# A two-layer encoder on one core: waits placed behind a branch's first gates, and the neighbourhood values in two matmul passes instead of three

## The chip, the cores and the metric

The kernel runs on one NeuronCore of a Trainium2 chip (trn2). The metric is the device time of one execution in microseconds, as a median of several runs. Before the change it is 1117.35 us, the median of three runs from 1117.09 to 1117.47 us. The lines L1 to L1314 named below are those of the kernel before; where a line of the changed kernel is meant, the text says so.

## The reference

A two-layer encoder works on 256 tokens of width 1024. Each layer is a hybrid mixer, a cross-attention to a memory of 256 tokens, and a feed-forward block with a depthwise convolution, with a layer norm behind each. The change lies in the mixer, which merges three branches, each weighed by its own sigmoid gate:

```python
    oa = diff_attention(qa..., ka..., va..., lam, pos)
    ya = (rms_norm(oa, subln_g) * (1.0 - lam_init)).transpose(0, 2, 1, 3).reshape(b, s, DA_V)
    yb = neighbourhood_attention(qb, kb, vb, rpb)
    yc = gb * dwconv(gc * hc, sc_conv_w)
    g = jax.nn.sigmoid(gates.reshape(b, s, N_BRANCH, D_MODEL))
    merged = (g[:, :, 0] * (ya @ w_branch[0]) + g[:, :, 1] * (yb @ w_branch[1])
              + g[:, :, 2] * (yc @ w_branch[2]))
    return merged @ w_mix_out
```

`neighbourhood_attention` has 8 heads of 64. The tokens are a grid of 4 rows by 64 columns; a query sees 16 columns of all four rows. The kernel computes it as full 256 by 256 scores for each head with a bias that holds a large negative number outside the window, a softmax, and the product with the head's values:

```python
        sc = jnp.where(mask, sc + bias[None].astype(jnp.float32), -jnp.inf)
        p = jax.nn.softmax(...)
        return jnp.einsum('bhjqrk,bhrjkd->bhjqd', p.astype(v_blk.dtype), v_blk)
```

## The kernel before

**High and low parts.** The inputs are float32, and TensorE multiplies them as float32r, a rounded form. To keep precision, operands are split into a high part (a copy to float32r on ScalarE, L276) and a low part (the rest, on VectorE, L277) by `split_from`, and a product is made of three matmuls that add up in PSUM (`mm3`, L271 to L273): high times high, high times low, low times high. The weights arrive as 355 units of 128 by 1024 float32 (`raw`), are loaded by SyncE's DMA queue, and are split in the same way into `hi` and `lo`, up to seven units ahead of their use (`LOOK`, 8 buffers each).

**What sets the order.** The program is written as steps (`Step`) by generators. A planner, `interleave`, puts them in one list: a main line of projections, side lines that are spawned (attention groups, `Spawn`), and waits (`Wait`) that hold the main line until a side line is done by the planner's own costs. The list is then recorded, and the tile framework's scheduler may still move instructions on each engine before it fixes their order; on the chip each engine issues its own list in that order. PSUM has three buffers `acc` for projections and five `att` for attention and transposes; a buffer is taken again when its last reader is done.

**The mixer.** In each layer the main line runs the values, queries and keys of both attentions and the convolution branch, and then three calls of `branch`: first the convolution branch (br 2), then the differential attention (br 0), then the neighbourhood (br 1). A call does two halves of 512 output columns: four weight units of gate projection (`g`, matmuls of 512 columns into two `acc` tiles, one for each 128 tokens; a tanh on ScalarE evacuates each, L830), then two units of the branch product (`w`, two more `acc` tiles), which VectorE merges with the gate (L838, and L841 for the later branches). Ahead of the call for branch 0 stands `Wait(da)`, ahead of that for branch 1 `Wait(na0..na3)`.

**The neighbourhood.** Four side lines `near_pair` (t = 0 to 3, two heads each) run while the main line is in the first `branch` call. Each has scores for two heads (L587 and L588, then on VectorE bias, maximum, and after the exponent on ScalarE the division by the sum, L744 to L753), two transposes of the weights (L761, then a split into the t512 tiles `t` by L276 and L277), and `values`: for each of two heads j and two token tiles k one `mm3` of the values' high and low parts (`vh`, `vl`, 128 columns that hold both heads) with the transposed weights (256 queries), 12 matmuls of 256 columns into one `att` tile `po`. Of its 128 rows those of head j are used, and split to `yb` from PSUM, 64 rows by 256 columns at a time (two L276 and two L277 a pair).

## Time and profile before

| what | number |
|---|---|
| median of three runs | 1117.35 us (1117.09 to 1117.47) |
| the profiled execution's own time | 1118.29 us |
| its span | 1116.5 us |
| PE busy | 1096.6 us, 98% of the span, 6684 matmuls |
| weight loads of PE (PEld) | 980.5 us, 88% |
| DVE (VectorE) busy | 831.6 us, 74%, 1300 instructions |
| ACT (ScalarE) busy | 643.2 us, 58%, 1062 instructions |
| mean granted TensorE clock | 0.996 |
| share of PE in the chain that ended last | 91% |

The profiled execution is 0.94 us longer than the median. A matmul is shown with its whole duration, and matmuls overlap, so the distance between two starts is what one costs the engine. Names such as `acc<-hi,big` give the tile written and the tiles read, `att<-t,big` is a value product, `lo<-raw,hi` the low part of a weight unit. Layer 1 of the model repeats layer 0 some 540 us later.

### The profile page before, as it was taken

Reading aid. Unit: us, or ns where it says so; the run is one execution under the profiler, and the core shown is the slowest. Engines: PE = TensorE matmul, PEld = TensorE weight load, DVE = VectorE, ACT = ScalarE, POOL = GpSimd, SP = SyncE. Lnnn points to the kernel's source line nnn. Section 1 sums busy time; section 2 is a strip of 40 time slices with the busy share of each in tenths; the row PEclk is TensorE's granted clock in tenths of the full one; section 3 lists DMA queues with packets and bytes.
Section 4 is the critical chain, followed back from the end, with each engine's and each line's share of the span. In section 5 each row is a group of like instructions: output and inputs, shape, how many; then the busy total and the mean of one; then the engine's idle time right before and its main releaser. Section 6 shows DMA issues by size and latency. Waiting matters only on the chain.

```text
span 1116.5 us, 17399 instructions
## 1 busy us (share of the span) xinstructions
PE 1096.6 (98%) x6684; PEld 980.5 (88%) x6684; DVE 831.6 (74%) x1300; ACT 643.2 (58%) x1062; POOL 12.3 (1%) x18
## 2 busy tenths in 40 slices
PE   9999999999999999999999999999999989999997
PEld 7899998888998988888889999888889978888886
DVE  7787888666974988885586888865787658988744
ACT  5656767445553676664445667654546436766540
POOL 0000000000000000000000000000000000000001
PEclk9999999999999999999999999999999989999999
DMA  7884437567463576666747544566756516766651
GB/s 301 283 257 148 147 129 234 176 200 246 152 207 97 166 238 190 189 189 194 262 147 216 185 157 171 170 188 197 236 170 195 164 44 225 214 190 188 194 173 38
DMA packets 60466, 208.45 MB, mean 187 GB/s; under 512 B 7008, under 2 KB 8288, under 8 KB 60384
## 3 DMA queue, kind: packets, MB, share of 16 engines
q1 hardware_dynamic: 59952, 206.83, 57.6%
q8 instruction: 52, 0.85, 0.3%
q10 hardware_dynamic: 432, 0.52, 0.1%
q14 instruction: 30, 0.25, 0.1%
HBM read 204.18 MB, written 1.05 MB: 184 GB/s over the span
## 4 chain that ended last, share of the span: by engine, by line
PE 91%; DVE 3%; DMA 2%; ACT 1%; SPq 1%; issue 1%; DVEq 0%; ACTq 0%
PE acc L271 18%; PE acc L272 18%; PE acc L273 18%; PE acc L303 12%; PE acc L301 7%; PE att L272 4%; PE att L273 4%; PE att L271 4%; PE acc L299 2%; DMA raw<-in_w_dram 1%; PE att L462 1%; DMA big<-in_emb_ln_b_dram 1%; DVE lo L277 1%; PE att L673 1%; PE att L588 1%
## 5 line engine op out<-in xcount | busy, mean ns | idle before, releaser
L277 DVE TENSOR_TENSOR lo<-raw,hi 128x1024 fp32r<-128x1024 f32 x355 | 432.1, 1223 | 179.3 <-ACT hi L276 173.6
L276 ACT CAST hi<-raw 128x1024 fp32r<-128x1024 f32 x355 | 371.2, 1052 | 221.7 <-PE acc L273 72.8
L272 PE MATMUL acc<-lo,big 128*128 128x512 f32 x584 | 229.5, 393 | 0.8 <-DVE lo L277 0.8
L271 PE MATMUL acc<-hi,big 128*128 128x512 f32 x584 | 229.0, 394 | 0.4 <-ACT hi L276 0.4
L273 PE MATMUL acc<-hi,big 128*128 128x512 f32 x584 | 227.0, 391 | 0.0
L271 PE MATMUL acc<-big,hi 128*128 128x256 f32 x704 | 200.5, 286 | 3.2 <-ACT big L335 2.4
L273 PE MATMUL acc<-big,lo 128*128 128x256 f32 x704 | 200.8, 285 | 0.6 <-DVE lo L277 0.6
L272 PE MATMUL acc<-big,hi 128*128 128x256 f32 x704 | 200.2, 285 | 0.2 <-DVE big L277 0.2
L303 PE MATMUL acc<-big,hi 128*128 128x512 f32 x588 | 149.4, 393 | 0.0
L271 PEld LDWEIGHTS acc<-big,hi 128*128 128x128 f32 x704 | 134.8, 192 | 4.4 <-ACT big L335 2.8
L273 PEld LDWEIGHTS acc<-big,lo 128*128 128x128 f32 x704 | 135.0, 192 | 1.2 <-DVE lo L277 1.0
L272 PEld LDWEIGHTS acc<-big,hi 128*128 128x128 f32 x704 | 135.0, 192 | 0.8 <-DVE big L277 0.4
L273 PEld LDWEIGHTS acc<-hi,big 128*128 128x128 f32 x584 | 109.8, 188 | 22.8 <-DVE big L277 0.2
L272 PEld LDWEIGHTS acc<-lo,big 128*128 128x128 f32 x584 | 110.0, 188 | 21.7 <-DVE lo L277 1.9
L271 PEld LDWEIGHTS acc<-hi,big 128*128 128x128 f32 x584 | 109.8, 188 | 20.9 <-ACT hi L276 1.0
L303 PEld LDWEIGHTS acc<-big,hi 128*128 128x128 f32 x588 | 105.1, 189 | 18.3
L301 PEld LDWEIGHTS acc<-big,lo 128*128 128x128 f32 x672 | 91.8, 191 | 6.6 <-ACT big L276 0.2
L301 PE MATMUL acc<-big,lo 128*128 128x256 f32 x672 | 94.0, 283 | 0.0
L272 PE MATMUL att<-lo,big 128*128 128x256 f32 (+1 forms) x228 | 73.8, 324 | 0.0
L271 PE MATMUL att<-hi,big 128*128 128x256 f32 (+1 forms) x228 | 73.5, 322 | 0.0
L273 PE MATMUL att<-hi,big 128*128 128x256 f32 (+1 forms) x228 | 73.4, 322 | 0.0
L307 ACT COPY t<-acc 128x256 f32<-128x256 f32 x84 | 31.1, 370 | 59.0 <-PE acc L303 59.0
(155 smaller groups left out, 1237.7 us busy)
## 6 DMA issues: line engine op xcount, KB each, us to landing
raw<-in_w_dram SPq DMA_DIRECT2D x355, 512.0 KB, 4.3
t<-in_bias_dram SPq DMA_DIRECT2D x16, 256.0 KB, 5.2
big<-in_ln_g_dram SPq DMA_DIRECT2D x6, 512.0 KB, 5.4
big<-in_ln_b_dram SPq DMA_DIRECT2D x6, 512.0 KB, 6.2
raw<-in_memT_dram SPq DMA_DIRECT2D x6, 512.0 KB, 4.7
big<-big SPq DMA_DIRECT2D x16, 128.0 KB, 2.3
x<-in_x_dram SPq DMA_DIRECT2D x4, 256.0 KB, 7.5
t<-in_memT_dram SPq DMA_DIRECT2D x3, 256.0 KB, 6.6
```

The lines of the kernel that those rows point to most:

```text
L271: mm(o, lh, rh, start=first, stop=False)
L272: mm(o, lh, rl, start=False, stop=False)
L273: self.done = mm(o, ll, rh, start=False, stop=last)
L276: return (self.nc.scalar.copy(ah, src), self.nc.vector.tensor_tensor(out=al, in0=src, in1=rd(ah), op=ALU.subtract))
L277: self.nc.vector.tensor_tensor(out=al, in0=src, in1=rd(ah), op=ALU.subtract))
L299: mm(o, hi[:, 0], xa.both(0), start=True, stop=False)
L301: mm(o[:, S:], lo[:, k], xa.hi(k), start=False, stop=False)
L303: mm(o, hi[:, k], xa.both(k), start=False, stop=k == KT - 1)
L307: self.nc.scalar.copy(dst, o[:, S:])
L462: nc.tensor.transpose(pt[:, k], self.x[i][:, (n * h + k) * P:(n * h + k + 1) * P], self.ident)
L588: self.nc.tensor.matmul(o, q[m][:, h, t], k[2 + m][:, h], start=False, stop=True)
L673: self.nc.tensor.matmul(sh["po"][:, hd], st["wt"][:, h, k], va[:, 512 * k + hd * P:512 * k + (hd + 1) * P], start=k == 0, stop=k == 1)
```

## The change

**The operand.** The values of the neighbourhood, `vb`, are evacuated into one tile for each 128 tokens, in which each head has 128 columns: its 64 high columns, then its 64 low ones. One matmul with such a block as the stationary operand gives the high part's product in rows 0 to 63 and the low part's in rows 64 to 127. `values` runs two passes for each j and k, one with the weights' high part and one with their low part: 8 matmuls a pair in place of 12. The product low times low, which was left out, is now included.

**The evacuation.** The two halves of `po` are to be added: ScalarE copies the lower 64 rows by 512 columns from PSUM to a new t512 tile `y` (L782 of the changed kernel), VectorE adds the upper ones (L783), and the split to `yb` then reads `y` in SBUF (L786 on ScalarE, L787 on VectorE, two each, 64 by 256). A pair's chain of evacuation is ACT, DVE, ACT, DVE, where it was ACT, DVE.

**The waits.** `Wait(da)` and `Wait(na...)` move from ahead of a `branch` call to behind its first four gate units. The planner's cost of `values` goes from 1.3 to 0.96, its latency from 1.6 to 2.4. Other lines of the changed kernel stand 2 to 8 lines lower (L761 is L763, L838 is L846, L830 is L836).

The planner's list has 561 steps in both kernels, and they stand in the same order. SyncE's and GpSimd's instructions stand in the same order too. What moves is the order on PE, ACT and DVE near the value products, and a little around the norm and the first feed-forward units of layer 1.

```diff
--- before.py
+++ after.py
@@ -371,7 +371,9 @@
             if n not in self.T or self.T[n][0] != l:
                 self.T[n] = (l, [self.big(F32R), self.big(F32R)] if split else self.big())
             if split:
-                self.split_from(o, self.T[n][1][0][:, sl], self.T[n][1][1][:, sl])
+
+                v = self.T[n][1][i].rearrange("p (h s d) -> p h s d", s=2, d=64)
+                self.split_from(o.rearrange("p (h d) -> p h d", d=64), v[:, :, 0], v[:, :, 1])
             else:
                 self.nc.scalar.copy(self.T[n][1][:, sl], o)
         return self.tok(n, l, 0, xn, evac, tiles)
@@ -769,21 +771,25 @@
             if ("yb", l) not in self.T:
                 self.T["yb", l] = self.big_act(1)
             yb = self.T["yb", l]
-            vh, vl = self.T["vb"][1]
+
             po = self.att().rearrange("p (j t) -> p j t", j=2)
             for j in range(2):
                 for k in range(2):
-                    c = slice(512 * k + t * P, 512 * k + (t + 1) * P)
-                    wh, wl = st["w"][j]
-                    self.mm3(po[:, j], vh[:, c], vl[:, c], wh[:, k], wl[:, k], k == 0, k == 1)
+                    v = self.T["vb"][1][k][:, (2 * t + j) * P:(2 * t + j + 1) * P]
+                    for s in range(2):
+                        nc.tensor.matmul(po[:, j], v, st["w"][j][s][:, k], start=k == s == 0, stop=k == s == 1)
+            y = self.t512().rearrange("p (j t) -> p j t", j=2)
+            nc.scalar.copy(y[:64], po[64:])
+            nc.vector.tensor_tensor(out=y[:64], in0=po[:64], in1=y[:64], op=ALU.add)
             for j in range(2):
                 a = slice(64 * j, 64 * j + 64)
-                self.split_from(po[a, j], yb.his[0][a, t], yb.los[0][a, t])
+                nc.scalar.copy(yb.his[0][a, t], y[:64, j])
+                nc.vector.tensor_tensor(out=yb.los[0][a, t], in0=y[:64, j], in1=rd(yb.his[0])[a, t], op=ALU.subtract)
 
         yield Step(scores, 0.87, 4.0, acq=2, rel=2)
         yield Step(lambda: transp(0), 0.44, 1.4, acq=1, rel=1)
         yield Step(lambda: transp(1), 0.44, 1.8, acq=1, rel=1)
-        yield Step(values, 1.3, 1.6, acq=1, rel=1)
+        yield Step(values, 0.96, 2.4, acq=1, rel=1)
 
 
     def conv_branch(self, l, xn):
@@ -817,7 +823,7 @@
         yield from self.feat("gb", l, 4, xn, gb)
 
 
-    def branch(self, l, br, y, xn, first=False, last=False):
+    def branch(self, l, br, y, xn, first=False, last=False, waits=()):
 
         T = self.T
         for q in range(2):
@@ -829,6 +835,8 @@
 
                 self.nc.scalar.activation(gs[i], o, AF.Tanh, scale=0.5)
             yield from self.tok(f"g{br}", l, q, xn, gate)
+            if q == 0 and waits:
+                yield Wait(*waits)
 
             def merge(i, o, gs=gs, sl=sl):
                 nc = self.nc
@@ -1032,10 +1040,8 @@
             for t in range(4):
                 yield Spawn(f"na{l}{t}", self.near_pair(l, t), 1.0)
             yield from self.branch(l, 2, ("yc", l), xn, first=True)
-            yield Wait(f"da{l}")
-            yield from self.branch(l, 0, ("ya", l), xn)
-            yield Wait(*(f"na{l}{t}" for t in range(4)))
-            yield from self.branch(l, 1, ("yb", l), xn, last=True)
+            yield from self.branch(l, 0, ("ya", l), xn, waits=[f"da{l}"])
+            yield from self.branch(l, 1, ("yb", l), xn, last=True, waits=[f"na{l}{t}" for t in range(4)])
             yield lnc(0)
             yield Allow(max(allow["v", l, 0], allow["k", l, 7]))
             yield Step(self.load_mem)
```

PE, layer 0, the last pair (t = 3): `att_2179` and `att_2206` before (`att_2176` and `att_2203` now) are the transposed weights of its two heads, `att_2233` (`att_2230`) its `po`, and `acc_2285` (`acc_2281`) the second tile of the product of branch 2's second half. First the kernel before, then the changed one.

```order
L761 MATMUL att_2179<-ident,t_1942 128x128 x4
L761 MATMUL att_2206<-ident,t_1944 128x128 x4
L271 MATMUL att_2233<-t_2184,big_920 128x256
L272 MATMUL att_2233<-t_2185,big_920 128x256
L273 MATMUL att_2233<-t_2184,big_921 128x256
L271 MATMUL att_2233<-t_2184,big_920 128x256
L272 MATMUL att_2233<-t_2185,big_920 128x256
L273 MATMUL att_2233<-t_2184,big_921 128x256
L271 MATMUL att_2233<-t_2211,big_920 128x256
L271 MATMUL acc_2285<-hi_1978,big_1439 128x512
L272 MATMUL acc_2285<-lo_1979,big_1439 128x512
```

```order
L763 MATMUL att_2176<-ident,t_1942 128x128 x4
L763 MATMUL att_2203<-ident,t_1944 128x128
L780 MATMUL att_2230<-t_2181,big_920 128x256
L763 MATMUL att_2203<-ident,t_1944 128x128 x3
L780 MATMUL att_2230<-t_2182,big_920 128x256
L780 MATMUL att_2230<-t_2181,big_921 128x256
L780 MATMUL att_2230<-t_2182,big_921 128x256
L780 MATMUL att_2230<-t_2208,big_920 128x256
L780 MATMUL att_2230<-t_2209,big_920 128x256
L780 MATMUL att_2230<-t_2208,big_921 128x256
L780 MATMUL att_2230<-t_2209,big_921 128x256
L271 MATMUL acc_2281<-hi_1978,big_1439 128x512
```

Before, the first head's products and one of the second stand ahead of 12 matmuls into `acc`, and the other five behind them; now all eight stand ahead of the `acc` matmuls, the first of them among the transposes.

ACT at the same place: `t_2262` and `t_2270` (`t_2258` and `t_2266` now) are the gates of branch 2's second half, read from the `acc` tiles of the gate projection.

```order
L276 CAST hi_2274<-raw_2272 128x1024
L276 CAST big_2036<-att_2162 64x256
L276 CAST t_2184<-att_2179 128x512
L276 CAST big_2036<-att_2162 64x256
L276 CAST t_2211<-att_2206 128x512
L830 ACTIVATE t_2262<-acc_2148 128x512
L830 ACTIVATE t_2270<-acc_2155 128x512
L276 CAST hi_2294<-raw_2292 128x1024
L276 CAST hi_2314<-raw_2312 128x1024
L276 CAST big_2036<-att_2233 64x256
```

```order
L276 CAST hi_2270<-raw_2268 128x1024
L782 COPY t_2169<-att_2160 64x512
L276 CAST t_2181<-att_2176 128x512
L786 CAST big_2036<-t_2169 64x256 x2
L276 CAST t_2208<-att_2203 128x512
L782 COPY t_2239<-att_2230 64x512
L836 ACTIVATE t_2258<-acc_2146 128x512
L836 ACTIVATE t_2266<-acc_2153 128x512
L786 CAST big_2036<-t_2239 64x256 x2
L276 CAST hi_2290<-raw_2288 128x1024
```

The two tanh stood behind the copy of the second transposed head; now the copy of the last pair's `po` stands ahead of them. `acc_2281` takes the PSUM buffer of `acc_2146`, as `acc_2285` took that of `acc_2148`.

DVE ahead of that: the last rows before the division of the last head's weights, `t_1944` (L753, now L755), and what follows.

```order
L277 TENSOR_TENSOR lo_2218<-raw_2215,hi_2217 128x1024
L753 TENSOR_SCALAR t_1942<-t_1942,s_2088 128x256 x2
L277 TENSOR_TENSOR lo_2253<-raw_2250,hi_2252 128x1024
L751 RECIPROCAL s_2103<-s_2103 128x2
L277 TENSOR_TENSOR lo_2275<-raw_2272,hi_2274 128x1024
L277 TENSOR_TENSOR big_2037<-att_2162,big_2036 64x256
L753 TENSOR_SCALAR t_1944<-t_1944,s_2103 128x256 x2
L277 TENSOR_TENSOR t_2185<-att_2179,t_2184 128x512
L277 TENSOR_TENSOR big_2037<-att_2162,big_2036 64x256
L277 TENSOR_TENSOR t_2212<-att_2206,t_2211 128x512
```

```order
L277 TENSOR_TENSOR lo_2215<-raw_2212,hi_2214 128x1024
L277 TENSOR_TENSOR lo_2249<-raw_2246,hi_2248 128x1024
L753 RECIPROCAL s_2101<-s_2101 128x2
L277 TENSOR_TENSOR lo_2271<-raw_2268,hi_2270 128x1024
L783 TENSOR_TENSOR t_2169<-att_2160,t_2169 64x512
L755 TENSOR_SCALAR t_1944<-t_1944,s_2101 128x256 x2
L277 TENSOR_TENSOR t_2182<-att_2176,t_2181 128x512
L787 TENSOR_TENSOR big_2037<-t_2169,big_2036 64x256 x2
L277 TENSOR_TENSOR t_2209<-att_2203,t_2208 128x512
L783 TENSOR_TENSOR t_2239<-att_2230,t_2239 64x512
```

From the weight unit `lo_2114` (`lo_2112` now) up to this division, five splits to `big_2037` stood ahead of it; now three adds (L783) and four splits (L787) do, the third add directly ahead of it. The five weight units and the other rows in between are the same in number. In the same stretch the merge of `acc_2022` (L838, now L846) has moved back: it stood two rows behind that weight unit and now stands six behind it.

## The prediction

> **What bounds the kernel now.** I read the page's busy line and chain first, then the groups by shape, then the stretch of the value products as a timeline.
>
> ```profile
> PE   1096.6 (98%) x6684; PEld 980.5 (88%) x6684; DVE 831.6 (74%) x1300; ACT 643.2 (58%) x1062; POOL 12.3 (1%) x18
> PE 91%; DVE 3%; DMA 2%; ACT 1%; SPq 1%; issue 1%; DVEq 0%; ACTq 0%
> ```
>
> PE is at work almost throughout, and nine tenths of the chain are PE. So a matmul taken away should shorten the end by its distance to the next one, as long as PE finds its operands and buffers ready. The averages hide that the stretch of the change has a second limit (stretch, PE, PEld, DVE, ACT and POOL busy with counts, clock, DMA):
>
> ```profile
> 177.12:190.02 12.90, 12.90 (x71) 11.01 (x70) 12.74 (x24) 8.03 (x17) 0.00 (x0) 1.00 0.62 194
> 717.12:730.01 12.89, 12.89 (x71) 11.01 (x70) 12.73 (x24) 8.03 (x17) 0.00 (x0) 1.00 0.60 193
> 196.00:230.00 34.00, 34.00 (x153) 28.18 (x153) 20.50 (x23) 16.15 (x19) 0.00 (x0) 1.00 0.61 186
> ```
>
> In the 12.9 us ahead of the last head's division DVE works 12.74 us: there it is as full as PE, in both layers to 0.01 us. Behind 196 us it is 60% busy. The end of that full stretch in layer 0, in time order (start, duration, engine):
>
> ```profile
> 187.11 0.28 PE L273 MATMUL att<-t,big 128*128 128x256 f32 x1
> 187.23 0.28 PE L271 MATMUL att<-t,big 128*128 128x256 f32 x1
> ...
> 189.89 1.33 PE L761 MATMUL att<-ident,t 128*128 128x128 f32 x8
> 190.02 0.59 DVE L753 TENSOR_SCALAR t<-t,s 128x256 f32<-128x256 f32 x2
> ...
> 191.20 0.69 DVE L277 TENSOR_TENSOR t<-att,t 128x512 fp32r<-128x512 f32 x1 [0.58 <-ACT t L276]
> ...
> 191.94 0.39 PE L272 MATMUL att<-t,big 128*128 128x256 f32 x1 [0.34 <-DVE t L277]
> ...
> 192.06 1.10 ACT L830 ACTIVATE t<-acc 128x512 f32<-128x512 f32 x2
> ...
> 192.38 0.69 DVE L277 TENSOR_TENSOR t<-att,t 128x512 fp32r<-128x512 f32 x1
> ...
> 192.77 0.45 PE L271 MATMUL acc<-hi,big 128*128 128x512 f32 x1
> ...
> 196.17 0.40 PE L271 MATMUL acc<-hi,big 128*128 128x512 f32 x1
> ```
>
> A 256-column matmul costs PE 0.12 us (187.11 to 187.23). From 192.77 to 196.17 PE runs twelve of 512 columns and five of 256: 3.40 less 0.60 leaves 2.8 us, 0.23 for one of 512. PE reaches the last pair's transposes at 189.89, just as DVE gets to the division at 190.02 which the second four of them need, and then waits for the low part of 191.20 (next matmul 191.94). PE and DVE arrive together; DVE has no slack to give. The second head's low part is done only at 193.07 (192.38 + 0.69), but five of its six matmuls come after the twelve of 512 columns, so that costs nothing now.
>
> **The change part by part.** The moved waits: nothing. The planner's list keeps its order, so at both places the awaited side line was done. In the trace the last transposes of `ya` in layer 1 start at 675.7, 60 us ahead of branch 0's gates (736.10 there, 196.17 in layer 0), and the last split of `yb` in layer 0 starts at 201.45, ahead of the merge at 229.90 that precedes branch 1.
>
> ```profile
> L714 PE MATMUL att<-ident,t x16: 270/272/273, 133.8 to 675.7; 128*128 128x128 f32 x16
> 201.45 0.43 DVE L277 TENSOR_TENSOR big<-att,big 64x256 fp32r<-64x256 f32 x1
> 229.90 0.68 DVE L838 SCALAR_TENSOR_TENSOR t<-t,acc 128x512 f32<-128x512 f32 x1
> ```
>
> Removed: 4 matmuls of 256 columns in each of 8 pairs, 32 x 0.12 = 3.84 us of PE, 1.92 a layer. The split of `vb` keeps its two instructions a tile at the same size; No row has its blocks of 64 columns. I take 0; were each as slow as a whole weight unit (1.22 us in place of 0.69), that would be 0.5 us an instruction, in a stretch where the convolution's twelve units still lie between it and its use; a gain there would be hidden in the same way.
>
> Added: a copy on ACT and an add on DVE, both 64 rows by 512, and the splits now read SBUF.
>
> ```profile
> L277 DVE TENSOR_TENSOR big<-att,big 64x256 fp32r<-64x256 f32 x16 | 6.7, 420 | 0.4
> L566 DVE TENSOR_TENSOR big<-acc,big 64x512 fp32r<-64x512 f32 x8 | 5.5, 688 | 0.2
> L574 ACT CAST big<-acc 64x512 fp32r<-64x512 f32 x8 | 4.7, 583 | 0.1
> ```
>
> The add is nearest to L566 (a PSUM and an SBUF operand, 688 ns), the copy to L574 (583 ns, also across partitions). The splits from SBUF I leave at the 420 ns of those from PSUM, since no row has that form; each stands one for one. On a full DVE an operation takes its distance to the next one's start:
>
> ```profile
> 175.99 1.22 DVE L277 TENSOR_TENSOR lo<-raw,hi 128x1024 fp32r<-128x1024 f32 x1
> 177.12 0.41 DVE L277 TENSOR_TENSOR big<-att,big 64x256 fp32r<-64x256 f32 x1
> 177.45 1.27 DVE L838 SCALAR_TENSOR_TENSOR big<-t,acc 128x512 f32<-128x512 f32 x2
> 178.65 0.67 DVE L746 TENSOR_REDUCE s<-t 128x2 f32<-128x512 f32 x1
> ...
> 183.74 1.21 DVE L277 TENSOR_TENSOR lo<-raw,hi 128x1024 fp32r<-128x1024 f32 x1
> 184.97 0.43 DVE L277 TENSOR_TENSOR big<-att,big 64x256 fp32r<-64x256 f32 x1
> ```
>
> That is 1.13 us for a weight unit (175.99 to 177.12), 0.33 for a split (177.12 to 177.45), 0.60 for 512 columns (two merges from 177.45 to 178.65). Usually an operation starts 0.09 us ahead of its predecessor's end (177.12 against 177.21); the split at 184.97 starts 0.02 behind it.
>
> Now along the new order, from the weight unit at 175.99, which nothing has moved yet. Ahead of the last division stand three adds more and one split less: 3 x 0.60 - 0.33 = 1.5 us. Three or four of the five splits there lose 0.11 us as at 184.97, and stand beside each other now; that may give 0.4 back. I take 1.1, so the division starts at 191.1 and its first half is done at 191.45. The bounds are 1.5 and, if an add of 64 rows cost a split's 0.33 in place of 0.60, 0.3. PE has meanwhile saved three pairs, 1.44 us, and loses most of it: the merge of `acc_2022`, whose buffer `acc_2153` needs, now stands behind an add, a maximum, a weight unit, a split and a bias (177.12 + 0.60 + 0.60 + 1.13 + 0.33 + 0.60) and ends near 181.1. From there PE has 36 matmuls of 512 columns, 7 of 256 and four transposes, 8.3 + 0.84 + 0.4 us, and is at the last transposes by 190.7. It stands until 191.45. These are the first waits, and the whole saving has gone into them.
>
> From there: three further transposes to 191.95; the low part of the first head (0.69 us of DVE behind the second division half, from 191.6) releases PE at 192.3; the second head's transposes are evacuated by ACT 192.3 to 192.9, its low part by DVE 192.9 to 193.6; PE runs its last three matmuls from 193.6 and ends at about 194.15. The cover of twelve matmuls, which before hid 193.07, is gone.
>
> Then the third wait. ACT's next instruction is the copy of this `po`, 194.2 to 194.8, and only behind it stands the tanh that frees the buffer of `acc_2281`: it ends at 195.3. Before, that tanh ran at 192.06 and was done at 192.67, and the `acc` matmul started at 192.77. So `acc_2281` starts at 195.36, takes its 2.8 us, and branch 0's gates start at 198.1 where they started at 196.17: 1.95 us later, though 16 matmuls were saved. Behind it nothing gives the time back or takes more: from 196 to 230 PE is busy 34.00 of 34.00 us, DVE has 13 us to spare, and weights are split seven units ahead, 7 x 2.8 = 19 us. Layer 1 has the same order and the same rows, so twice 1.95 = 3.9 us.
>
> The reordered feed-forward units and norms of layer 1 I take at 0 with 1 us either way: the same matmuls and buffers, and the large wait there hangs on PE's own last projection. It has its price beside it:
>
> ```profile
> 912.90 1.11 PE L462 MATMUL att<-ident,x 128*128 128x128 f32 x4 [3.74 <-DVE x L426]
> 913.00:919.00 6.00, 6.00 (x29) 6.00 (x30) 5.25 (x9) 4.46 (x7) 0.00 (x0) 0.50 0.10 10
> 86.00:88.20 2.20, 1.02 (x8) 0.77 (x6) 2.17 (x3) 2.14 (x4) 0.00 (x0) 1.00 0.59 207
> 88.20:92.00 3.80, 3.78 (x31) 3.79 (x32) 2.69 (x5) 1.03 (x5) 0.00 (x0) 1.00 0.35 116
> ```
>
> Sum: 1118.29 + 3.9 = 1122.2 for a profiled execution; the runs' median lies 0.94 below it, so 1121.2 us.
>
> **Rivals.** (a) All is hidden and PE keeps its 3.84 us: 1113.5 us. PE's 98% speaks for it, and that the products end 0.48 us sooner in each pair; DVE's 12.74 of 12.90 us speaks against. It would need DVE's three adds to find 1.5 us of room in that stretch, which has 0.16.
>
> (b) The first two waits come, the third doesn't, since ACT's copy finds `po` done in time: `acc_2281` then starts at 194.15, gates at 196.95, 0.8 a layer: 1117.35 + 1.6 = 1118.9 us, no change that can be told. For it stands that each step above may be some tenths early or late; against it, that the tanh stands behind the copy in ACT's own list, and the copy behind PE's last matmul.
>
> (c) The clock drops. Behind the wait of 3.74 us at 912.90 the granted clock is 0.50 for 6 us, which costs half of them; behind some 1.2 us ahead of 88.20 (PE busy 1.02 of 2.20) it stays at 1.00. My four new waits in 16 us, for a merge, a division, a low part and a tanh, are 1.4, 0.75, 0.7 and 1.2 us long, each of the harmless kind; if they counted together, 3 us a layer would be added: 1127 us. [...]
>
> **How the numbers follow.** Runs of this kernel differ by some tenths of a us; under 0.2%, 2.2 us, I call no change. Forecast 0.62, (a) 0.13, (b) 0.19, (c) 0.06. Slower is forecast and (c): 0.68; same is (b): 0.19; faster is (a): 0.13. The forecast's own range is 1119.5 to 1123.0: DVE's bounds move it by 0.8 down or 0.4 up a layer, and layer 1's other rows by up to 1 either way. The given range takes (b) in and leaves out (a) and most of (c): 1116.0 to 1124.0 us.
>
> **What would show it.** Right: the last L755 of each layer starts near 1 us later than 190.02 and 730.01; the L782 of the last pair stands directly ahead of the tanh and that tanh ends behind 195; the first `acc` matmul behind it waits for ACT; the gates of branch 0 start near 198; PE's busy time is lower and its idle time higher. Wrong: the tanh near 192, L783 well under 0.6 us, PE starting branch 0's gates ahead of 196, or the granted clock below 1.00 between 180 and 200.

## The result, and the profile after

The changed kernel takes 1127.88 us (median of 4 runs, 1126.39 to 1128.07) where the kernel before takes 1117.41 in the same job: a ratio of 1.0084, interval 1.0072 to 1.0096, 10.5 us slower. The forecast was slower, 1121.2 us in a range of 1116.0 to 1124.0. The sign was right; the loss is well over twice the 3.9 us forecast, and the time lies outside the range.

The profiled execution is the shortest of the four (1126.39 us; its span is 1124.6 us against 1116.5). The busy line and the chain of waits of the changed kernel:

```profile
PE 1097.6 (98%) x6652; PEld 979.8 (87%) x6652; DVE 836.1 (74%) x1308; ACT 649.6 (58%) x1070; POOL 12.3 (1%) x18
PE 91%; DVE 5%; ACT 1%; DMA 1%; issue 1%; SPq 0%; DVEq 0%; ACTq 0%
```

32 matmuls are gone (6652 for 6684), and yet PE's busy time, forecast to be lower, went up by 1.0 us: the remaining matmuls took longer. DVE's share of the chain went from 3 to 5%.

To place the loss, the span is cut at the transposes of `x` behind a norm (L462, now L464), which stand in both kernels at the same point of PE's order. For layer 1, of the kernel before and of the changed kernel (start, duration, engine):

```profile
568.65 0.38 PE L462 MATMUL att<-ident,x 128*128 128x128 f32 x2
...
829.66 0.38 PE L462 MATMUL att<-ident,x 128*128 128x128 f32 x2
```

```profile
574.18 0.38 PE L464 MATMUL att<-ident,x 128*128 128x128 f32 x2
...
838.89 0.38 PE L464 MATMUL att<-ident,x 128*128 128x128 f32 x2
```

From one landmark to the other, the stretch with branches and attention, is 261.01 us before and 264.71 after, +3.70. In layer 0, from the second of the two transposes that start at 35.95 (now 37.52) to the first of those at 289.76 (now 295.32), it is 253.70 and 257.69, +3.99. Ahead of it stand +1.57 (the first 38 us, where weights' DMAs land 1 us later in this execution and PE's clock halves for 3.4 us; a later run of the old products, e14 below, had 1.25 of it with the same half clock, so it isn't the change's). Behind layer 1 stand -1.1 (behind the 3.7 us wait for the norm the clock stays halved for 3.41 us, where it was 6.83). Sum 8.1 us, the difference of the spans. The other three runs are 1.3 to 1.7 us longer than the profiled one; they have no trace, so where that lies was not seen.

Now the stretch in layer 0 of the changed kernel as a timeline. For comparison with the kernel before, take 1.57 us off.

```profile
182.33 0.50 PE L271 MATMUL acc<-hi,big 128*128 128x512 f32 x1 [0.79 <-DVE big L846]
...
192.59 0.60 DVE L755 TENSOR_SCALAR t<-t,s 128x256 f32<-128x256 f32 x2
...
192.98 0.33 PE L763 MATMUL att<-ident,t 128*128 128x128 f32 x1 [0.88 <-DVE t L755]
...
195.34 0.62 PE L780 MATMUL att<-t,big 128*128 128x256 f32 x3 [0.45 <-DVE t L277]
196.00 0.58 ACT L782 COPY t<-att 64x512 f32<-64x512 f32 x1 [1.54 <-PE att L780]
196.61 1.09 ACT L836 ACTIVATE t<-acc 128x512 f32<-128x512 f32 x2
...
197.26 0.50 PE L271 MATMUL acc<-hi,big 128*128 128x512 f32 x1 [1.29 <-ACT t L836]
...
198.55 0.63 PE L272 MATMUL acc<-lo,big 128*128 128x512 f32 x1
198.98 0.63 PE L273 MATMUL acc<-hi,big 128*128 128x512 f32 x1
...
201.70 0.40 PE L271 MATMUL acc<-hi,big 128*128 128x512 f32 x1
```

The four waits of the forecast are there: for the merge, the division, the low part and the tanh, the last behind L782 on ACT. Counted as the distance to the next matmul beyond its usual spacing, the waits (with one of 0.35 us beside the merge's) come to 4.61 us, where there was one of 0.61. But behind the last of them the 512-column matmuls stand 0.43 us apart (198.55 to 198.98) in place of 0.23, until the last one ahead of the gates. The reason is in the windows view (stretch, PE, PEld, DVE, ACT and POOL busy with counts, granted clock, DMA), cut into 3.41 us:

```profile
191.14:194.55 3.41, 2.41 (x16) 1.59 (x14) 3.38 (x7) 1.96 (x4) 0.00 (x0) 1.00 0.89 323
194.55:197.96 3.41, 1.67 (x7) 1.19 (x8) 2.02 (x4) 1.93 (x4) 0.00 (x0) 1.00 0.29 117
197.96:201.37 3.41, 3.41 (x10) 2.65 (x9) 1.49 (x3) 1.47 (x3) 0.00 (x0) 0.50 0.00 0
...
737.27:740.68 3.41, 2.04 (x11) 1.20 (x10) 2.02 (x5) 1.49 (x4) 0.00 (x0) 1.00 0.72 256
740.68:744.09 3.41, 2.93 (x7) 2.35 (x8) 1.99 (x4) 1.61 (x4) 0.00 (x0) 0.50 0.00 0
```

The granted clock is 0.50 for 3.41 us behind the value products, in both layers: one of the signs by which the forecast said it would know itself wrong. Branch 0's gates start at 201.70, less 1.57 200.1, where 198.1 was forecast. Layer 0 adds up: 4.00 us more of waits, some 1.7 for half of 3.41 us, less 1.92 for the matmuls saved, 3.8 of the 3.99 measured.

### The profile page after: what moved, and what is told of

It reads as the page before. It is cut to its first block, busy times and chain, and to the rows that moved or that the text cites. A ratio compares the mean times of both kernels' runs of the same rounds, so it can differ in the third digit from the quotient of the medians.

```text
span 1124.6 us, 17355 instructions
## 1 busy us (share of the span) xinstructions
PE 1097.6 (98%) x6652; PEld 979.8 (87%) x6652; DVE 836.1 (74%) x1308; ACT 649.6 (58%) x1070; POOL 12.3 (1%) x18
## 3 DMA queue, kind: packets, MB, share of 16 engines
HBM read 204.18 MB, written 1.05 MB: 182 GB/s over the span
## 4 chain that ended last, share of the span: by engine, by line
PE 91%; DVE 5%; ACT 1%; DMA 1%; issue 1%; SPq 0%; DVEq 0%; ACTq 0%
PE acc L271 18%; PE acc L272 18%; PE acc L273 18%; PE acc L303 12%; PE acc L301 7%; PE att L272 4%; PE att L271 4%; PE att L273 4%; PE acc L299 2%; DVE lo L277 1%; DMA raw<-in_w_dram 1%; PE att L464 1%; PE att L675 1%; PE att L590 1%; PE att L589 1%
## 5 line engine op out<-in xcount | busy, mean ns | idle before, releaser
L271 PEld LDWEIGHTS acc<-hi,big 128*128 128x128 f32 x584 | 111.1, 190 | 27.3 <-ACT t L836 3.0
L273 PEld LDWEIGHTS acc<-hi,big 128*128 128x128 f32 x584 | 111.1, 190 | 23.3
```

Of the source, the lines that this page charges most:

```text
L271: mm(o, lh, rh, start=first, stop=False)
L273: self.done = mm(o, ll, rh, start=False, stop=last)
```

## The experiments

In every kernel the layers' legs between the landmarks are compared, since they leave out what differs between executions at the start and behind layer 1. Each leg is of one profiled execution; the times are medians. The last column says how long the granted clock was 0.50 within the two legs, near the value products.

| kernel | time, us | layer 0 leg | layer 1 leg | half clock, us |
|---|---|---|---|---|
| before | 1117.4 | 253.70 | 261.01 | none |
| the change | 1127.88 | 257.69 | 264.71 | 3.4 in both layers |
| e1 filler | 1123.85 | 256.06 | 265.89 | 3.4 in layer 1 |
| e2 last values later | 1119.29 | 254.46 | 263.09 | 3.4 in layer 1 |
| e3 no copy and add | 1117.01 | 254.25 | 260.10 | 3.4 in layer 0 |
| e4 longer latencies | 1128.91 | 258.41 | 266.43 | 6.8 in both layers |
| e5 pairs 12 us apart | 1117.34 | 255.23 | 259.15 | none |
| e6 the same, old products | 1116.21 | 253.32 | 259.96 | none |
| e7 pairs 16 us apart | 1117.82 | 253.70 | 260.91 | none |
| e8 low parts on POOL | 1123.82 | 258.25 | 264.70 | 6.8 in layer 0, 3.4 in layer 1 |
| e9 divisions first, values later | 1117.63 | 252.96 | 260.13 | none |
| e10 divisions first | 1123.96 | 256.13 | 264.40 | 3.4 in both layers |
| e11 divisions first, old products | 1115.40 | 252.52 | 259.88 | none |
| e12 all divisions first, values later | 1120.14 | 255.29 | 261.15 | 3.4 in layer 0 |
| e13 as e9, tanh first | 1114.33 | 251.28 | 258.60 | none |
| e14 divisions and tanh first, old products | 1115.49 | 252.52 | 259.85 | none |
| e15 all three edits, old products | 1115.20 | 252.55 | 259.88 | none |
| e16 all three edits, the change | 1112.77 | 251.26 | 258.60 | none |

The moved waits have no run of their own: the old kernel with them alone has, on every engine, the same instructions with the same buffers and waits in the same order as the kernel before.

### Is it the clock? (e1)

```diff
                     for s in range(2):
+                        for r in range(5 if t == 3 and j == 1 and k == s == 0 else 0):
+                            nc.tensor.matmul(po[:, j], v, st["w"][j][s][:, k], start=True, stop=True)
                         nc.tensor.matmul(po[:, j], v, ...)
```

> The second head's first value matmul of the last pair is issued five times more (each overwrites the same result), ahead of the wait of 0.71 us for that head's low part: 0.6 us of PE work in an idle stretch, in both layers; nothing else moves. Theory A (the waits themselves come to 4.0 us a layer, less 1.92 saved; the rest of the loss is the clock, which falls where PE is busy less than about a third of one window of 3.41 us): the emptiest window goes from 0.30 busy to 0.48, the granted clock stays at 1.00 behind the value products, some 1.5 us come back in each layer, 1124.8 us. Theory B (the slow matmuls behind the waits come from the last wait of 1.45 us alone, or the clock looks at single idle times): the clock falls as before and the time stays at 1127.9 us, or rises by up to 1 us.

Measured: 1123.85 us (1122.43 to 1124.79), 4.0 us under the change, by adding 10 matmuls. The windows of layer 0 and layer 1, at the phase of this execution:

```profile
193.71:197.12 3.41, 2.12 (x13) 1.73 (x13) 2.00 (x4) 2.13 (x5) 0.00 (x0) 1.00 0.26 106
197.12:200.53 3.41, 3.41 (x17) 2.81 (x16) 2.22 (x4) 2.33 (x3) 0.00 (x0) 1.00 0.00 0
...
739.84:743.25 3.41, 3.41 (x10) 2.64 (x9) 1.27 (x4) 1.67 (x3) 0.00 (x0) 0.50 0.00 0
```

In layer 0 the clock stays at 1.00, PE runs 17 matmuls in the window behind the products in place of 10, and the leg is 1.63 us shorter, with the other waits unchanged (1.29 us for the tanh as before). In layer 1 it fell in this execution, the slowest of the four, and that leg is 1.18 us longer than the change's; one wait in it, for a cast ahead of the products, is 0.9 us longer. So the clock is a cause of its own, worth some 1.6 us a layer, and layer 0 speaks against theory B: its wait of 1.29 us for the tanh is as long as before, and the clock stays. Two falls are worth 3.3 us; of the other 0.7 us between the medians no trace tells, though the change's profiled execution also lost 1.1 us ahead of layer 0 that this one didn't. That two different waits in one window, of 0.45 and 1.29 us, bring the clock down is what the forecast had priced at nothing.

### Where do the waits come from? (e2, e3, e4)

```diff
-        yield Step(lambda: transp(1), 0.44, 1.8, acq=1, rel=1)
+        yield Step(lambda: transp(1), 0.44, 1.8 if t < 3 else 4.5, acq=1, rel=1)    # e2
```

> The last pair's value step is listed one weight unit later (its transposes' latency 4.5 in place of 1.8), so that ACT's copy L782 stands behind the two tanh that free the accumulators. Theory A (the third and the longest wait is ACT's order): the waits of 0.71 and 1.45 us at the end go, that of 0.35 + 1.05 for the merge and that of 1.05 for the division stay; the clock stays at 1.00; per layer 2.45 us of waits against 0.61 before and 1.92 saved, so about 1117.2 us. Theory B (DVE is too full; whatever stands behind the value products waits for it): the waits only move, the time lies between 1121 us (clock kept) and 1128 us.

Measured: 1119.29 us (1117.83 to 1120.71), a ratio to before of 1.0011, interval 1.0001 to 1.0020. The tanh comes at 194.14, ahead of the copy, and the matmul behind it at 194.80, with 0.38 us beyond its spacing in place of 1.45; the division's wait (0.90 us idle) and the merge's stay, as expected by theory A. Layer 0 kept its clock, layer 1 lost it. (This execution, at 1120.71 us, is the slowest of the ten.) So ACT's order made the third wait, and with the clock it is worth most of the loss. The median is 2 us above theory A's 1117.2, which had the clock at 1.00 in both layers.

```diff
-            y = self.t512().rearrange("p (j t) -> p j t", j=2)                      # e3
-            nc.scalar.copy(y[:64], po[64:])
-            nc.vector.tensor_tensor(out=y[:64], in0=po[:64], in1=y[:64], op=ALU.add)
...
-                nc.scalar.copy(yb.his[0][a, t], y[:64, j])
+                nc.scalar.copy(yb.his[0][a, t], po[:64, j])
```

> The copy L782 and the add L783 are left out, and the splits read the upper 64 rows of the PSUM result: the product of the values' low part is left out of the output. Everything else of the change stays, the 16 matmuls fewer per layer too. Theory A (copy and add make the loss; the fewer matmuls would be a gain): faster than the kernel before, up to 1113.6 us where all 3.84 us are kept. Theory B (DVE was full before already, so PE only reaches the last division sooner and waits there): 1117.4 us less the 0.5 us or so by which the last products end sooner, 1116.4 to 1117.4 us.

Measured: 1117.01 us (1115.26 to 1117.88), ratio 0.9990, interval 0.9980 to 0.9999, within theory B's range: even without copy and add most of the 3.84 us doesn't show. The timeline of this kernel, and its windows at the phase of its execution:

```profile
189.36 0.61 DVE L755 TENSOR_SCALAR t<-t,s 128x256 f32<-128x256 f32 x2
...
189.76 0.81 PE L763 MATMUL att<-ident,t 128*128 128x128 f32 x4 [0.41 <-DVE t L755]
...
190.90 0.72 PE L763 MATMUL att<-ident,t 128*128 128x128 f32 x4 [0.33 <-DVE t L755]
...
192.24 0.72 PE L780 MATMUL att<-t,big 128*128 128x256 f32 x3 [0.50 <-DVE t L277]
...
189.20:192.62 3.42, 2.18 (x13) 1.43 (x13) 3.24 (x10) 2.31 (x6) 0.00 (x0) 1.00 0.91 346
192.62:196.03 3.41, 3.41 (x12) 2.73 (x11) 0.94 (x2) 0.87 (x3) 0.00 (x0) 0.50 0.10 42
```

PE gets to the divisions sooner and waits for both, as the forecast had read it ("DVE has no slack to give"). But the waits are only a part: in layer 0 this kernel lost the clock too, and its leg is 0.55 us longer than before; in layer 1, with the same three waits and the clock at 1.00, it is 0.91 us shorter. So about half of the saving does show where the clock stays.

> The whole change, with the planner told of longer latencies in a pair's steps: scores 6.5 in place of 4.0, first transposes 2.6 for 1.4, second 2.6 for 1.8, so that the pairs are spread over more weight units (the last values one unit later) and DVE's work on them too. Theory A (the copies and adds fit, if the attention isn't packed into 13 us): most waits go, the clock stays at 1.00, 1113.6 to 1116 us. Theory B (the chain from product to split is too long at any spacing, since banks and buffers are held longer): waits for banks instead, 1119 us or more.

The edit is in the same three lines, 6.5, 2.6 and 2.6 for 4.0, 1.4 and 1.8. Measured: 1128.91 us (1127.39 to 1129.57), theory B's side, though not for banks. In layer 0 PE stands 3.21 us for one low part, which DVE starts at 191.58, behind a weight unit and the splits of two products (rows not shown), and the clock is halved for two intervals, 6.83 us, in both layers:

```profile
188.45 0.66 PE L780 MATMUL att<-t,big 128*128 128x256 f32 x4
192.31 0.39 PE L780 MATMUL att<-t,big 128*128 128x256 f32 x1 [3.21 <-DVE t L277]
```

### Is it DVE's sum of work? (e5 to e8)

```diff
-                yield Spawn(f"na{l}{t}", self.near_pair(l, t), 1.0)
+                yield Spawn(f"na{l}{t}", self.near_pair(l, t), 1.0 + 12.0 * t)      # 16.0 in e7
```

> The whole change, and the four pairs of a layer start 12 us of the planner's time apart in place of together (the last values six weight units later). Theory A (the loss is DVE's full stretch: copies, adds and splits of four pairs beside the weights' low parts; spread wide, they fit in DVE's idle 40%): the waits of 0.35 to 1.45 us near the value products go, the clock stays at 1.00, and all 3.84 us of matmuls are kept, with the wait of 0.61 us a layer that the kernel before had: 1112.5 to 1114.5 us. Theory B (each product's chain, PE to ACT to DVE to ACT to DVE, makes PE wait at any spacing, or the buffers held longer do): 1119 us or more.

> The kernel before, with its twelve matmuls a pair and without copy and add, and the pairs 12 us apart. Theory A: only its wait of 0.61 us a layer can go, 1116.2 to 1117.4 us, so that the change is worth about 3.8 us where DVE has room. Theory B: the same spacing gains or loses as much here as with the change.

> As the stagger of 12 us, with 16 us (the last values ten weight units later than in the change, beside the second half of branch 0's gates). Theory A: as at 12 us or up to 1 us better, 1112.5 to 1114 us, since DVE has 43% for weights' low parts and some 7 us a pair. Theory B: worse than at 12 us, since buffers are held longer.

Measured: 1117.34, 1116.21 and 1117.82 us. Wide spacing takes the change's loss away (ratio 0.9998, interval 0.9989 to 1.0007) and the clock stays at 1.00 in both layers, but the 3.84 us do not come: the change stays 1.1 us behind the old products at the same spacing. By the legs it loses 1.91 us to them in layer 0 and gains 0.81 in layer 1. In layer 0 three waits over 0.5 us are left in e5, for a tanh, a division and a cast; in layer 1, 0.34 us idle is the longest. The longest is for the tanh:

```profile
177.57 0.62 PE L780 MATMUL att<-t,big 128*128 128x256 f32 x3
179.63 0.50 PE L271 MATMUL acc<-hi,big 128*128 128x512 f32 x1 [1.44 <-ACT t L836]
```

Neither theory holds as put: room on DVE is not enough. At 16 us (e7) it is no better, and theory A's 1112.5 to 1114 us are missed as well.

```diff
-                nc.vector.tensor_tensor(out=yb.los[0][a, t], in0=y[:64, j], ...)
+                (nc.vector if j else nc.gpsimd).tensor_tensor(out=yb.los[0][a, t], in0=y[:64, j], ...)
```

> The whole change, packed as it is, with the first head's low part of each pair (L787, j = 0) taken from DVE to POOL, which is idle there: four of DVE's eight splits a layer, 4 x 0.33 = 1.3 us, three of them ahead of the last division. Theory A (DVE's order and fullness set the last division, and the waits of 1.05, 0.71 and 1.45 us follow from it): the division comes 0.7 to 1.0 us sooner, the waits ahead of the last products shrink by that, and with them the clock's fall may go: 1123 to 1126.5 us. Theory B (the order on ACT and the merge set the waits, not DVE's load): no change, 1127.9 us; or worse, where POOL's split is slow and holds what waits for it.

Measured: 1123.82 us (1123.25 to 1126.05), inside theory A's range, but not for its reason, as far as the one profiled execution shows, the slowest of the four. The clock fell there in both layers. The merge's wait has gone, yet the last division comes only 0.2 us sooner (191.36 less 0.53 for this execution's start, against 192.59 less 1.57), and PE stands longer ahead of it (1.76 us beyond its spacing, for 1.05). DVE's rows of that kernel say why:

```profile
187.30 3.49 DVE L277 TENSOR_TENSOR lo<-raw,hi 128x1024 fp32r<-128x1024 f32 x3
190.70 0.16 DVE L753 RECIPROCAL s<-s 128x2 f32<-128x2 f32 x1
```

Three weight units stand in a row ahead of the last reciprocal: the room that the splits left went to work that isn't due for some 19 us (an estimate: seven units of 2.8 us). That points to the order on DVE, not the sum alone; e9 to e16 test it. The changed kernel has the same picture, with the last exponential read out by 189.22:

```profile
188.52 2.35 DVE L277 TENSOR_TENSOR lo<-raw,hi 128x1024 fp32r<-128x1024 f32 x2
...
189.03 0.19 ACT L751 ACTIVATION_READ_ACCUMULATOR t<-t,s 128x1 f32 x1
...
190.79 0.16 DVE L753 RECIPROCAL s<-s 128x2 f32<-128x2 f32 x1
190.86 1.21 DVE L277 TENSOR_TENSOR lo<-raw,hi 128x1024 fp32r<-128x1024 f32 x1
```

The reciprocal starts 1.57 us behind its operand, and the division (192.59) stands behind another weight unit and an add.

### The order on DVE (e9 to e12)

The kernel has a helper that holds weight splits behind a marked instruction of the same engine (`urgent` and `behind`, L279 to L287); it is used here on the divisions of the last pair (of all pairs in e12).

```diff
-                    nc.vector.tensor_scalar_mul(b[:, i], b[:, i], sx[:, i:i + 1])
+                    d = nc.vector.tensor_scalar_mul(b[:, i], b[:, i], sx[:, i:i + 1])
+                    if t == 3:                       # e9, e10, e11; without this line in e12
+                        self.urgent(d)
...
-        yield Step(lambda: transp(1), 0.44, 1.8, acq=1, rel=1)
+        yield Step(lambda: transp(1), 0.44, 1.8 if t < 3 else 4.5, acq=1, rel=1)    # e9, e12
```

> The whole change, with the weights' low parts that are listed after the last pair's scores held behind that pair's divisions on DVE (order on one engine, no wait), and the last pair's values listed one weight unit later. Theory A (not DVE's sum of work but its order makes the waits: in the change two weight units of 1.13 us each stood between the last exponentials, done at 189.2, and the last division, and others ahead of the merge that frees an accumulator): the last division comes 2 to 3 us sooner, the waits for the merge, the division, the low part and the tanh all but go, the clock stays, and most of the 3.84 us is kept: 1113.5 to 1116 us. Theory B (DVE's sum of work is the limit): what is put behind comes too late in its turn, PE waits for weights' low parts within the next seven units, 1118 us or more.

> As the one before, without the later listing of the last values: ACT's copy of the last product still stands ahead of the two tanh. Theory A: the division's wait goes, the tanh's wait (1.45 us, less what the products end sooner) stays, so about 1 us a layer above the one before: 1115.5 to 1118 us, the clock at 1.00. Theory B: 1120 us or more.

> The kernel before with the same order on DVE (weights' low parts behind the last pair's divisions). Theory A: only its 0.61 us a layer can go: 1116 to 1117.4 us. Theory B: slower than 1117.4 us, for weights that come late.

> As the first, with the divisions of all four pairs ahead of the weights' low parts that are listed after them. Theory A: no worse than the first, up to 1 us better where the earlier pairs' DVE work still stands behind weights (the merge at 181): 1113 to 1116 us. Theory B: weights' low parts late in the whole stretch, 1118 us or more.

Measured: 1117.63 (1115.19 to 1119.59), 1123.96, 1115.40 and 1120.14 us. With the change all three lie above theory A's ranges. On the old products (e11) the order alone gains, 0.6 us more than theory A's range had: ratio 0.9977, interval 0.9967 to 0.9987, and no wait over 0.25 us is left in the stretch. With the change, e9 has one wait left in each layer, and its rows show the chain:

```profile
184.92 0.61 DVE L755 TENSOR_SCALAR t<-t,s 128x256 f32<-128x256 f32 x2
185.46 4.62 DVE L277 TENSOR_TENSOR lo<-raw,hi 128x1024 fp32r<-128x1024 f32 x4
...
190.30 1.04 ACT L276 CAST hi<-raw 128x1024 fp32r<-128x1024 f32 x1 [0.61 <-DMA raw<-in_w_dram]
...
191.26 1.08 ACT L838 ACTIVATE t<-acc 128x512 f32<-128x512 f32 x2
...
191.90 0.50 PE L271 MATMUL acc<-hi,big 128*128 128x512 f32 x1 [2.08 <-ACT t L838]
```

The division is there at 184.92, 6 us sooner than in the change (theory A named 2 to 3). The four weight units that were put behind it follow in a row until 190.08, ACT's cast waits 0.61 us for the DMA of its weights, and the tanh stands behind the cast. That the weights land late because those units release their raw buffers late is the author's reading of this order; no row shows it. The wait has only moved, as theory B had it, though PE waits for a tanh behind a late cast and not for a low part. In e10, where the copy of the last product stands ahead of the tanh too, it costs the clock in both layers. In e12 PE waits some 2.5 us for the same tanh in each layer, and the clock falls in layer 0.

### One more order, and both products under it (e13 to e16)

```diff
+                th = self.nc.scalar.activation(gs[i], o, AF.Tanh, scale=0.5)
+                if first and sl.start:
+                    self.tc.add_manual_dep(self.cast.ins, th.ins.name, NOSYNC, reason="behind the gate")
```

`self.cast` is the last weight cast on ACT listed so far; it is held behind the tanh (order only), at the second half of branch 2's gates alone, where the expectation speaks of each half. The other two edits are those of e9 (in e14 that on the divisions alone).

> As the run with the last divisions first and the last values later, and besides the weight cast on ACT that is listed just ahead of the first tanh pair of each gate half of branch 2 stands behind it (order on ACT, no wait). In that run one wait was left in the stretch, of 2.2 us in each layer: the tanh stood behind a weight's cast, which waited for its weights' DMA, which waited for a raw buffer that DVE's postponed low parts freed late. Theory A (with that wait gone the change keeps its fewer matmuls): the wait shrinks to 0.5 us or less, 1113.0 to 1114.5 us, faster than the old products in the same order by 1 to 2 us. Theory B (whatever order, four adds more a layer on DVE cost what 16 matmuls save): another wait takes its place, 1115.4 us or more.

> The kernel before with the same two orders (last divisions ahead of the weights' low parts on DVE, tanh ahead of the weight's cast on ACT). Theory A: as with the first order alone, 1115.4 us, since no wait over 0.25 us was left in that stretch; the change with the same orders lies 1 to 2 us under it. Theory B: the same as the change or below it.

> The kernel before with all three edits of order that the fastest kernel so far has: last divisions first on DVE, tanh ahead of the weight's cast on ACT, and the last values listed one weight unit later, which the run with the old products lacked. Theory A: the later listing moves nothing there, 1115.0 to 1116.0 us as without it, and the change's products gain 1 to 2 us in the same order. Theory B: the later listing is what gained, and the old products reach 1114.3 us too.

> The same three edits with the change's products, once more, on the same chip and in the same rounds as the old products. Theory A: 1113.3 to 1114.8 us, 1 to 2 us below them. Theory B: no difference that can be told, under 0.5 us.

Measured: 1114.33 us (ratio to before 0.9964, interval 0.9951 to 0.9976) and 1115.49 us (0.9978, interval 0.9969 to 0.9988); in the second job, with all three edits on both, 1112.77 us for the change's products (0.9957, interval 0.9945 to 0.9969) and 1115.20 for the old ones (0.9976, interval 0.9967 to 0.9986). Theory A, both times: the change's products are 1.2 us faster in the first job and 2.4 in the second, where e16 even lies 0.5 us below the range named. PE's rows in e16: 0.42 us idle is all that is left of the four waits.

```profile
189.72 0.28 PE L782 MATMUL att<-t,big 128*128 128x256 f32 x1
190.42 0.50 PE L271 MATMUL acc<-hi,big 128*128 128x512 f32 x1 [0.42 <-ACT t L838]
```

And the landmarks of layer 1 in e16, then in e15:

```profile
566.56 0.38 PE L464 MATMUL att<-ident,x 128*128 128x128 f32 x2
...
825.16 0.38 PE L464 MATMUL att<-ident,x 128*128 128x128 f32 x2
```

```profile
567.75 0.38 PE L462 MATMUL att<-ident,x 128*128 128x128 f32 x2
...
827.63 0.38 PE L462 MATMUL att<-ident,x 128*128 128x128 f32 x2
```

258.60 against 259.88, 1.28 us a layer, 1.29 in layer 0. The matmuls saved are 1.92 us, and the wait that is left costs 0.57 beyond its spacing: 1.35. So the change is worth its matmuls once the orders on DVE and ACT let PE run, and the later listing of the last values gives the old products nothing (1115.20 for 1115.49). The change with the three edits is the fastest kernel of the study, 4.3 parts in a thousand under the kernel before.

## Why the prediction was wrong, and where it was right

- **The moved waits at nothing, PE's saving of 1.92 us a layer, the split of `vb` in blocks of 64 at nothing**: right. The group with the splits of `vb` keeps 684 ns on DVE (686 before), and the saving shows in e16 to within 0.1 us.
- **The prices of copy, add and splits**: right. The changed kernel's groups by shape, the mean in ns behind the busy time:

```profile
L787 DVE TENSOR_TENSOR big<-t,big 64x256 fp32r<-64x256 f32 x16 | 6.7, 416 | 0.4
L783 DVE TENSOR_TENSOR t<-att,t 64x512 f32<-64x512 f32 x8 | 5.4, 679 | 2.7 <-ACT t L782 2.7
L782 ACT COPY t<-att 64x512 f32<-64x512 f32 x8 | 4.7, 584 | 3.2 <-PE att L780 3.1
```

  Forecast were 420, 688 and 583.
- **The division**: forecast 1.1 us later, measured 192.59 less 1.57 less 190.02, 1.00 us; in layer 1 0.95.
- **The four waits**: right in place, order and cause; forecast 1.4, 0.75, 0.7 and 1.2 us, measured 1.40, 1.05, 0.71 and 1.45. The tanh behind L782 was forecast to let the `acc` matmul start at 195.36; it did at 197.26 less 1.57, 195.69. All waits and the saving together were to cost 1.95 us a layer; the waits measured 4.00 us more than before, less 1.92, so 2.08.
- **The step that failed** is the clock, rival (c). The forecast took each wait by itself, "each of the harmless kind", because 1.2 us of idle at 86 to 88 us had left the clock at 1.00, put it at 0 in the sum and gave its falling a chance of 0.06. It fell in both layers and cost some 1.7 us in the first and a little less in the second. The row that served as proof was cut at 86.00 and 88.20; counted as in the last section, the interval of the clock there, 86.17 to 89.58, has PE at work for 0.55 of it, against 0.30 behind the value products. Without the fall the profiled execution would have come out at 1123.1 us, next to the 1122.2 forecast for it. The rival's 1127 us came out near the time by luck: it priced 3 us a layer from 6 us at half clock, and a fall lasts 3.41 us here.
- **The rest of the distance** was not forecast either. Of the 6.7 us by which the time was missed, 4.2 lie between the profiled execution (1126.39) and its forecast (1122.2): some 3.3 for the clock, 0.3 for the waits, and 1.57 less 1.1 outside the two stretches. The other 2.4 come from which execution was profiled: the old kernel's stood 0.94 above its median, the change's 1.5 below. So the clock alone doesn't explain the whole miss: the median less 3.3 us is 1124.6, still just above the range. What made the other three executions of the changed kernel longer stays open.
- **Rival (a)**, all hidden, was rejected for DVE's 12.74 of 12.90 us, and e3's waits bear that out in this order. But "DVE is full" was half the reason. Weight units that are due up to seven units later stood ahead of the division in DVE's order; with the order changed in both kernels, e16 lies 2.4 us below e15, of the 3.84.

No idle time of PE in the interval ahead of either fall was over 1.3 us: 0.45 and 1.29 us in layer 0, 0.44 and part of another 1.29 in layer 1. Here the clock fell behind a few short waits within 3.41 us.

## What to carry to other kernels

Price short waits by the stretch they stand in, not one by one: add up PE's work in 3.4 us, and where it is under some two fifths, put a halved clock for the next 3.4 us into the sum (in these traces 30 of 30 intervals with a share under 0.37 were followed by one, two of five between 0.37 and 0.43, and none above). When a stage's second engine is "full", look at what it is full of: work that isn't due yet, ordered ahead of the chain that PE waits for, is slack, as long as what it holds, in e9 by the author's reading the raw buffers, isn't missed. And try a saving on PE together with the order that lets it through, or it shows as a loss, as it did here.

## What was not expected of the hardware

In these traces the granted clock changes on a fixed grid of 3.413 us. In the changed kernel's profile the half-clock intervals begin at 13.64, 197.96, 740.68 and 921.59 us: 184.32, 542.72 and 180.91 us apart, which is 54.0, 159.0 and 53.0 times 3.413. Cut on such a grid, the traces of the kernel before, the change and e1 to e14 have 5225 windows, and each shows a clock of 1.00 or of 0.50, none a value between.

What the falls go with in these traces is the share of the interval that PE works; whether all of its work counts alike was not tested. Counted from all 18 traces (each matmul at its usual spacing, 0.227, 0.12 and 0.11 us for 512, 256 and 128 columns, or until the next one starts), of 5721 intervals at full clock the 30 with a share under 0.37 were all followed by half clock, of 5 between 0.37 and 0.43 two were, and of 5686 above none. (Counted from each trace's first clock record, at 4 to 7 us, up to 1100 us. Ahead of that record the windows view gives 1.00, but the transposes of 128 columns stand 0.213 us apart there in place of 0.11, as they do at half clock behind 912.90 in the kernel before, so those intervals are left out.) With the way back it is alike: of 38 intervals at half clock in the windows of the 16 kernels named above, up to 1100 us, the 8 with PE busy for 0.62 to 0.79 of the interval were followed by another, the 30 with 0.84 and more were not. A share is not a length of idle time: the change's 0.30 is made of two waits, of 0.45 and 1.29 us, and in e1's layer 0 the wait of 1.29 us is as long, PE has 13 matmuls in the interval in place of 7, and the clock stays. A kernel can lose the clock in one layer and keep it in the other, as e1, e2, e3 and e12 did; each kernel has one trace, so whether that changes from one execution to the next was not seen. The limit near 0.4 is read off these traces alone; two cases between 0.37 and 0.43 fell and three did not, so it isn't sharper than that.
